# The last norm of a two-layer encoder: tiles read back from DRAM, and a last projection that gives rows

## The chip, the core and the metric

One Trainium2 chip, of which the program uses one core. The metric is the time of one execution in device microseconds. Of the core's engines, TensorE (PE, with its weight loads as PEld) multiplies, VectorE (DVE), ScalarE (ACT) and GpSimd (POOL) work on elements, and SyncE (SP) issues most transfers.

## The reference, cut to what matters

Two groups of sequences, one of 256 and one of 1024 tokens of 1024 features, get 16 learned tokens in front and pass through two layers with shared weights; everything is float32. What matters here is the second half of a layer and the end:

```
h = h + conv_ffn(rmsnorm(h, norm_ffn_g[layer]), w_up[layer], conv_w, conv_b, w_down[layer])
...
def conv_ffn(h, w_up, conv_w, conv_b, w_down):      # D_FF = 2816
    u = dwconv(h @ w_up, conv_w, conv_b, 1)         # width 3, along the tokens
    a, g = u[..., :D_FF], u[..., D_FF:]
    return (gelu(g) * a) @ w_down
...
h = rmsnorm(h, final_norm_g)                        # after the last layer, over the 1024 features
return h[:, N_META:]                                # the 16 learned tokens are dropped
```

## The kernel before

All tokens of both groups lie in one row of 1316 columns, and the residual `h` is kept transposed: features on partitions, in 8 blocks of 128, tokens along the free axis. Its home in DRAM is `hsp` (128 x 8 x 1316). A matmul in float32 is made of three in a rounded format (`mm3`, L237): high times high, high times low, low times high, each operand having been split into a high and a low part.

`ffn` (L301) runs once a layer, and `last` marks the second. It takes the tokens in two halves (`s`), each of two quarters, `ca` and `cb`, of 328 or 330 columns (`QO`, L59). The up projection of a block of two 128-wide strips and two quarters is done with seven products in place of eight (`pair`, L430; 12 matmuls a product, L456); POOL and ACT prepare the sums of weights and split them (`part`, `supply`, L331 to L367), eight products ahead. `inputs` (L373) prepares the token side for a whole half, in tiles of the pool `xs` (seven buffers). In a half, the first two pairs run interleaved (L568 to L577); `take` (L539) fetches the two quarters' residual tiles `hs` there. Then come ten turns, f0 = 2 to 20 (L579): a pair of the first kind (`hold`), `down` for the two strips before in both quarters, the load of the next two `w_down` units (`down_units`, L510), and a pair of the second kind (`gate`), which makes the activations `xa`.

`down` (L519) takes slices of `w_down` as the stationary operand and activations as the moving one: for each of the 8 feature blocks six matmuls of 328 or 330 columns into one of the PSUM banks a, b, c, d (two buffers each, taken in turn), and VectorE adds the result to `hs` (L526). After the turns, one `down` for each quarter is still due (`end`, L562). In the first layer `give` (L544) then stores `hs` to `hsp` from ACT's queue; in the second it does nothing. The first layer's second half also fetches its first half back (`again`, L548), for the next norm.

The final norm is done by jobs (`final`, L620) of up to 128 tokens, three a quarter: 8 transposes from `hs` into two banks (L632), two squares with sums on ACT (L635), the sum and the inverse root on DVE and POOL (L636, `rstd` L193), two scalings on DVE (L640) and a store from SP (L642). The scaled rows go into `hs` itself, over columns that were just transposed; a job of fewer than 128 tokens uses the columns of the job before (`home`, L1652 to L1653). The four quarters' jobs run at four places: quarter 0 between blocks of the first half's last `down` (L604), quarter 1 among the interleaved pairs of the second half (L567, L573), quarter 2 between blocks of the very last `down` (L610), quarter 3 after it (L611).

The order on TensorE is the program's (L1710 opens a manual schedule for it); the other engines' and SP's orders come from the scheduler's own timing of the program, which may put an instruction ahead of others that are written earlier.

Of the kernel before, what the change touches and what calls it, by code (L numbers as in the profile page):

```python
# [91 lines left out]
class Trunk:  # L92
# [208 lines left out]
    def ffn(self, l, p_norm, hn, h1, right):  # L301
# [242 lines left out]
        def give(c):  # L544
            if not last:
                self.store(self.hsp[:, :, QO[c][0]:QO[c][0] + QO[c][1]], hs[c][:, :, :QO[c][1]], True)
# [16 lines left out]
        for s in range(2):  # L563
# [3 lines left out]
            jobs = iter(self.final(fg, hs, (1,), "cd") if s and last else ())  # L567
            for i in range(7):  # L568
                for j, product, follow in pairs:
                    step(product, j, i)  # L570
                    follow(i)
                if i < 3:
                    next(jobs, lambda: None)()  # L573
                if i == 1:
                    take(ca)
                if i == (3 if s else 1):
                    take(cb)  # L577
            down_units(0)
            for f0 in range(2, NF, 2):  # L579
# [7 lines left out]
                elif s and not last and f0 in (6, 10):  # L587
                    behind = {2: [call(hfactors, f0 // 4 - 1)], 5: [call(hspread, f0 // 4 - 1)]}
                run_pair(ja, s, X, hold, behind)
# [7 lines left out]
            if not s:  # L597
# [6 lines left out]
                down(end, cb, {m: [f] for m, f in zip((1, 4, 7), self.final(fg, hs, (0,), "ab"))} if last else {})  # L604
                give(cb)
        left.close()
        if last:
            down(end, ca)
            fg = self.final_weights(self.wsp, "wlo")
            down(end, cb, {m: [f] for m, f in zip((1, 4, 7), self.final(fg, hs, (2,), "ab"))})  # L610
            for f in self.final(fg, hs, (3,), "ab"):  # L611
                f()
            return
# [1006 lines left out]
    def final(self, fg, hs, quarters, banks):  # L1620


        nc, v = self.nc, self.nc.vector

        def job(c, x, home, out, t, n):
            y = hs[c][:n, :, home:home + 128]
            ss = self.nrm.tile([128, 4], F32, tag="ss", name="ss", bufs=2)
            halves = []
            for g in range(2):
                ps = self.bank(banks, (128, 4, 128))  # L1630
                for k in range(4):
                    nc.tensor.transpose(ps[:n, k, :], hs[c][:, 4 * g + k, x:x + n], self.ident)
                halves.append(ps[:n])
            for g in range(2):
                nc.scalar.activation(out=y[:, 4 * g:4 * g + 4], in_=halves[g], func=AF.Square, accum_out=ss[:n, g:g + 1])
            v.tensor_tensor(out=ss[:n, 2:3], in0=ss[:n, 0:1], in1=ss[:n, 1:2], op=ALU.add)
            self.rstd(ss[:n, 3:4], ss[:n, 2:3])
            for g in range(2):
                q = slice(4 * g, 4 * g + 4)
                v.scalar_tensor_tensor(out=y[:, q], in0=halves[g], scalar=ss[:n, 3:4],  # L1640
                                       in1=fg[:n].rearrange("p (k x) -> p k x", x=128)[:, q], op0=ALU.mult, op1=ALU.mult)
            self.dma(out[0, t:t + n, :].rearrange("t (k x) -> t k x", x=128), y)

        jobs = []
        for c in quarters:
            c0, n = QO[c]
            home = None
            for col, out, count in ((COLA + NM, self.o["out_0"], TA - NM), (COLB + NM, self.o["out_1"], TB - NM)):
                a, b = max(col, c0), min(col + count, c0 + n)
                for x in range(a, b, 128):  # L1650
                    m = min(128, b - x)
                    if home is None or m == 128:  # L1652
                        home = x - c0  # L1653
                    jobs.append(lambda c=c, x=x - c0, home=home, out=out, t=x - col, m=m: job(c, x, home, out, t, m))
        return jobs
# [89 lines left out]
```

## Time and profile before

| | us |
|---|---|
| median of 3 executions | 3126.32 (3125.46 to 3127.15) |
| the profiled execution | 3126.3 |
| its span, first to last instruction | 3124.2 |
| TensorE busy in the span | 2830.4 (91%) |
| VectorE, ScalarE, GpSimd busy | 2031.4, 1505.7, 1704.5 |
| mean granted TensorE clock | 0.955 |

The rows that follow the change come from several views of this one execution. In a timeline a row is one instruction or several alike in sequence: start, length, engine, line of the kernel, operation, tile written and tiles read, shape; behind it, in brackets, how long the engine stood idle before it and what ended that. A matmul's length includes its drain, which the next one overlaps, so that the price of one in a stream is the distance between two starts. In the table of stretches, the columns are the length, then for each engine the busy time and the number of instructions, the granted clock as a share of the full one, the DMA engines' busy share and the GB/s.

### The profile page before, as it was taken

The numbers are of one execution on the slowest core, as the hardware profiler recorded it, in microseconds if no ns is written. First come the engines' busy times: TensorE is split into PE (matmuls) and PEld (weight loads), VectorE is DVE, ScalarE is ACT, GpSimd is POOL, SyncE is SP. The second block draws the span as 40 slices with busy tenths as digits, with TensorE's granted clock in tenths as the row PEclk, the third lists the DMA queues.
The fourth block names the chain that finished last, engine by engine and source line by source line (L and its number), as shares of the span: only waits on it lengthen the run. The fifth ranks groups of instructions, "written<-read, shape, count | busy, mean of one in ns | idle before, by whom it ended". The sixth has DMA issues, their size and how long they took to land. (4 is left out here: it accounts for less than half of the span.)

```text
span 3124.2 us, 48747 instructions
## 1 busy us (share of the span) xinstructions
PE 2830.4 (91%) x17937; PEld 2712.1 (87%) x17937; DVE 2031.4 (65%) x4210; ACT 1505.7 (48%) x2909; POOL 1704.5 (55%) x1438
## 2 busy tenths in 40 slices
PE   6999757879999989999989998897999996999995
PEld 5988536879999989999978887787999996999995
DVE  8998793256666686666664777757655566666663
ACT  5445782244444454444444666634444444444442
POOL 1000100068888877788714333327888884788871
PEclk9999877989999999999999999998999998999997
DMA  5332543242222252222247667664222223222211
GB/s 146 85 87 57 129 124 116 76 134 75 81 82 82 82 180 84 68 77 80 75 129 168 142 145 158 158 186 156 80 77 79 80 85 107 85 82 82 82 55 49
DMA packets 407693, 320.22 MB, mean 102 GB/s; under 512 B 39262, under 2 KB 384270, under 8 KB 407454
## 3 DMA queue, kind: packets, MB, share of 16 engines
q1 hardware_dynamic: 357502, 260.01, 29.0%
q0 software_dynamic: 35520, 32.89, 5.3%
q10 hardware_dynamic: 14432, 24.20, 2.2%
q8 instruction: 142, 2.33, 0.3%
q14 instruction: 97, 0.79, 0.1%
HBM read 257.82 MB, written 57.11 MB: 101 GB/s over the span
## 5 line engine op out<-in xcount | busy, mean ns | idle before, releaser
L516 POOL TENSOR_TENSOR dl<-rawd,dh 128x1024 fp32r<-128x1024 f32 x88 | 213.3, 2424 | 311.5 <-ACT dh L515 311.4
L248 PE MATMUL ps_a<-hh,whi 128*128 128x438 f32 (+5 forms) x848 | 295.2, 348 | 43.7 <-ACT hh L1160 27.1
L515 ACT CAST dh<-rawd 128x1024 fp32r<-128x1024 f32 x88 | 92.3, 1048 | 436.4 <-PE ps_d L249 421.2
L249 PE MATMUL ps_a<-hl,whi 128*128 128x438 f32 (+5 forms) x848 | 290.2, 342 | 3.0 <-DVE hl L1504 2.3
L253 PE MATMUL ps_a<-hh,wlo 128*128 128x438 f32 (+5 forms) x848 | 288.7, 341 | 0.0
L338 POOL TENSOR_TENSOR s<-raw 128x512 f32<-128x512 f32 x184 | 257.6, 1402 | 29.9 <-PE ps_d L253 25.4
L365 POOL TENSOR_TENSOR wlo<-s,wlo 128x512 fp32r<-128x512 f32 x176 | 235.7, 1340 | 16.5 <-ACT wlo L364 15.1
L365 POOL TENSOR_TENSOR whi<-s,whi 128x512 fp32r<-128x512 f32 x176 | 235.2, 1346 | 3.8 <-ACT whi L364 3.8
L364 ACT CAST wlo<-s 128x512 fp32r<-128x512 f32 x176 | 108.9, 620 | 229.5 <-PE ps_a L456 97.0
L248 PEld LDWEIGHTS ps_a<-hh,whi 128*128 128x128 f32 x848 | 165.1, 195 | 55.4 <-ACT hh L1160 27.8
L365 POOL TENSOR_TENSOR whi<-raw,whi 128x512 fp32r<-128x512 f32 x132 | 176.2, 1336 | 65.3 <-ACT whi L364 65.2
L456 PE MATMUL ps_c<-x,wlo 128*128 128x330 f32 (+1 forms) x1152 | 195.3, 319 | 11.1 <-DVE hs L1640 7.5
L456 PE MATMUL ps_a<-x,whi 128*128 128x330 f32 (+1 forms) x1104 | 187.6, 319 | 11.7 <-DVE x L1513 4.5
L456 PE MATMUL ps_d<-x,whi 128*128 128x330 f32 (+1 forms) x1104 | 188.1, 319 | 6.8 <-DVE x L1513 3.0
L456 PEld LDWEIGHTS ps_c<-x,wlo 128*128 128x128 f32 x1152 | 181.7, 193 | 11.9 <-issue 7.7
L456 PE MATMUL ps_d<-x,wlo 128*128 128x330 f32 (+1 forms) x1008 | 171.7, 320 | 15.9 <-ACT wlo L364 6.7
L456 PEld LDWEIGHTS ps_a<-x,whi 128*128 128x128 f32 x1104 | 174.5, 192 | 13.0 <-DVE x L1513 5.0
L456 PEld LDWEIGHTS ps_d<-x,whi 128*128 128x128 f32 x1104 | 174.5, 192 | 8.7 <-DVE x L1513 3.6
L456 PEld LDWEIGHTS ps_d<-x,wlo 128*128 128x128 f32 x1008 | 159.6, 193 | 18.3 <-ACT wlo L364 7.3
L456 PE MATMUL ps_a<-x,wlo 128*128 128x330 f32 (+1 forms) x1008 | 169.2, 317 | 5.0 <-DVE hs L1640 4.2
L365 POOL TENSOR_TENSOR wlo<-raw,wlo 128x512 fp32r<-128x512 f32 x132 | 171.6, 1312 | 1.4 <-ACT wlo L364 1.3
L249 PEld LDWEIGHTS ps_a<-hl,whi 128*128 128x128 f32 x848 | 164.7, 194 | 8.7 <-DVE hl L1504 2.6
(498 smaller groups left out, 8769.0 us busy)
## 6 DMA issues: line engine op xcount, KB each, us to landing
raw<-in_w_up SPq DMA_DIRECT2D x176, 512.0 KB
rawd<-in_w_down SPq DMA_DIRECT2D x88, 512.0 KB
qs<-st SPq DMA_DIRECT2D x48, 219.0 KB
q<-qs POOLq DMA_DIRECT2D x80, 128.0 KB, 3.8
raw<-in_w_out_ab SPq DMA_DIRECT2D x16, 512.0 KB
raw<-in_w_o SPq DMA_DIRECT2D x16, 512.0 KB
hs<-hsp SPq DMA_DIRECT2D x6, 1312.0 KB
raw<-in_w_in_ab SPq DMA_DIRECT2D x12, 512.0 KB
```

Of the source, the lines that this page charges most:

```text
L248: yield nc.tensor.matmul(ps, ah, bh, start=(j == 0), stop=False)
L249: yield nc.tensor.matmul(ps, ah, bl, start=False, stop=False)
L253: yield nc.tensor.matmul(ps, al, bh, start=False, stop=(j == n - 1))
L338: nc.gpsimd.tensor_tensor(out=out, in0=a, in1=b, op=op)
L364: nc.scalar.copy(w[:, 0], src)
L365: nc.gpsimd.tensor_tensor(out=w[:, 1], in0=src, in1=w[:, 0].bitcast(F32), op=ALU.subtract)
L456: nc.tensor.matmul(ps[b], w[:, e, k * 128:(k + 1) * 128], x[:, f, k, :n], start=(opens and k == 0 and y == 0), stop=(k == 3 and y == 2), s ...
L515: nc.scalar.copy(hi, raw)
L516: nc.gpsimd.tensor_tensor(out=lo, in0=raw, in1=hi.bitcast(F32), op=ALU.subtract)
```

## The change

- `give` stores in the second layer too, so that after the first half quarters 0 and 1 go to `hsp`, as in the first layer. No norm job runs in the last `down` of the first half or among the interleaved pairs.
- In the second half six jobs, for the tiles of quarters 0 and 1, run one a turn in turns f0 = 4 to 14, after the last product of the first pair. A job fetches its tile from `hsp` into a part of a free `xs` tile, transposes it into banks a and b, and finishes as before (`finish`); its scaled rows go into another part of the same tile.
- The last `down` is not called in the second half. In its place, for each tile of up to 128 tokens of quarters 2 and 3, and for each half of the features, the activations are the stationary operand and a `w_down` unit is the moving one, 512 columns at a time, so that rows of tokens come out; four products of `hs` with the identity add the residual into the same bank. Then `finish` works from the banks, with its result in a tile of its own in `wsp` (four buffers).
- `final_norm_g` is loaded once.

```diff
--- before.py
+++ after.py
@@ -542,8 +542,7 @@
             self.dma(hs[c][:, :, :QO[c][1]], self.hsp[:, :, QO[c][0]:QO[c][0] + QO[c][1]])
 
         def give(c):
-            if not last:
-                self.store(self.hsp[:, :, QO[c][0]:QO[c][0] + QO[c][1]], hs[c][:, :, :QO[c][1]], True)
+            self.store(self.hsp[:, :, QO[c][0]:QO[c][0] + QO[c][1]], hs[c][:, :, :QO[c][1]], True)
 
         def again(c):
 
@@ -564,13 +563,12 @@
             j0 = len(up) * s
             ca, cb = 2 * s, 2 * s + 1
             pairs = [(j0, *pair(j0, s, X, hold)), (j0 + 1, *pair(j0 + 1, s, X, gate))]
-            jobs = iter(self.final(fg, hs, (1,), "cd") if s and last else ())
+
+            jobs = iter(self.final(fg, (0, 1), xtile().rearrange("p a k n -> p (a k n)").bitcast(F32)) if s and last else ())
             for i in range(7):
                 for j, product, follow in pairs:
                     step(product, j, i)
                     follow(i)
-                if i < 3:
-                    next(jobs, lambda: None)()
                 if i == 1:
                     take(ca)
                 if i == (3 if s else 1):
@@ -586,6 +584,8 @@
                     again(f0 // 4 - 1)
                 elif s and not last and f0 in (6, 10):
                     behind = {2: [call(hfactors, f0 // 4 - 1)], 5: [call(hspread, f0 // 4 - 1)]}
+                elif s and last and f0 > 2:
+                    behind = {6: [next(jobs, lambda: None)]}
                 run_pair(ja, s, X, hold, behind)
                 down(f0 - 2, ca)
                 down(f0 - 2, cb)
@@ -601,16 +601,23 @@
                 X = inputs(first, ya, yb, 332, tuple(gated))
                 down(end, ca)
                 give(ca)
-                down(end, cb, {m: [f] for m, f in zip((1, 4, 7), self.final(fg, hs, (0,), "ab"))} if last else {})
+                down(end, cb)
                 give(cb)
+        if last:
+            for c in (ca, cb):
+                for x, out, t, n in self.rows(c):
+                    halves = []
+                    for g in range(2):
+                        ps = self.bank("abcd")[:n]
+                        q = slice(512 * g, 512 * g + 512)
+                        self.mm3(ps, [(*(a[:, x:x + n] for a in acts[y, c % 2]), *(u[:, q] for u in units[end + y])) for y in range(2)],
+                                 [(ps[:, 128 * k:128 * k + 128], hs[c][:, 4 * g + k, x:x + n], self.ident) for k in range(4)])
+                        halves.append(ps.rearrange("p (k x) -> p k x", k=4))
+                    y = self.wsp.tile([128, 1024], FR, tag="whi", name="y").bitcast(F32)
+                    self.finish(fg, halves, y[:n].rearrange("p (k x) -> p k x", k=KD), out, t, n)
+            left.close()
+            return
         left.close()
-        if last:
-            down(end, ca)
-            fg = self.final_weights(self.wsp, "wlo")
-            down(end, cb, {m: [f] for m, f in zip((1, 4, 7), self.final(fg, hs, (2,), "ab"))})
-            for f in self.final(fg, hs, (3,), "ab"):
-                f()
-            return
         self.split_tiles(pool(hn, "hn1"))
 
         def apply(c):
@@ -1617,42 +1624,44 @@
         self.dma(fg, self.i["final_norm_g"].rearrange("(o d) -> o d", o=1).to_broadcast([128, D]))
         return fg
 
-    def final(self, fg, hs, quarters, banks):
-
+    def rows(self, c):
+
+        c0, n = QO[c]
+        for col, out, count in ((COLA + NM, self.o["out_0"], TA - NM), (COLB + NM, self.o["out_1"], TB - NM)):
+            a, b = max(col, c0), min(col + count, c0 + n)
+            for x in range(a, b, 128):
+                yield x - c0, out, x - col, min(128, b - x)
+
+    def finish(self, fg, halves, y, out, t, n):
 
         nc, v = self.nc, self.nc.vector
-
-        def job(c, x, home, out, t, n):
-            y = hs[c][:n, :, home:home + 128]
-            ss = self.nrm.tile([128, 4], F32, tag="ss", name="ss", bufs=2)
+        ss = self.nrm.tile([128, 4], F32, tag="ss", name="ss", bufs=2)
+        for g in range(2):
+            nc.scalar.activation(out=y[:, 4 * g:4 * g + 4], in_=halves[g], func=AF.Square, accum_out=ss[:n, g:g + 1])
+        v.tensor_tensor(out=ss[:n, 2:3], in0=ss[:n, 0:1], in1=ss[:n, 1:2], op=ALU.add)
+        self.rstd(ss[:n, 3:4], ss[:n, 2:3])
+        for g in range(2):
+            q = slice(4 * g, 4 * g + 4)
+            v.scalar_tensor_tensor(out=y[:, q], in0=halves[g], scalar=ss[:n, 3:4],
+                                   in1=fg[:n].rearrange("p (k x) -> p k x", x=128)[:, q], op0=ALU.mult, op1=ALU.mult)
+        self.dma(out[0, t:t + n, :].rearrange("t (k x) -> t k x", x=128), y)
+
+    def final(self, fg, quarters, room):
+
+
+        h, y = (room[:, a:a + 1024].rearrange("p (k x) -> p k x", k=KD) for a in (0, 1280))
+
+        def job(c, x, out, t, n):
+            self.dma(h[:, :, :n], self.hsp[:, :, QO[c][0] + x:QO[c][0] + x + n])
             halves = []
             for g in range(2):
-                ps = self.bank(banks, (128, 4, 128))
+                ps = self.bank("ab", (128, 4, 128))
                 for k in range(4):
-                    nc.tensor.transpose(ps[:n, k, :], hs[c][:, 4 * g + k, x:x + n], self.ident)
+                    self.nc.tensor.transpose(ps[:n, k, :], h[:, 4 * g + k, :n], self.ident)
                 halves.append(ps[:n])
...
-        jobs = []
-        for c in quarters:
-            c0, n = QO[c]
-            home = None
-            for col, out, count in ((COLA + NM, self.o["out_0"], TA - NM), (COLB + NM, self.o["out_1"], TB - NM)):
-                a, b = max(col, c0), min(col + count, c0 + n)
-                for x in range(a, b, 128):
-                    m = min(128, b - x)
-                    if home is None or m == 128:
-                        home = x - c0
-                    jobs.append(lambda c=c, x=x - c0, home=home, out=out, t=x - col, m=m: job(c, x, home, out, t, m))
-        return jobs
+            self.finish(fg, halves, y[:n], out, t, n)
+
+        return [lambda c=c, r=r: job(c, *r) for c in quarters for r in self.rows(c)]
 
     def mix(self, es):
 
```

## Rows read from the trace of the kernel before

**Rows 1.** The head of the page: busy time by engine, and TensorE in 40 slices.

```profile
PE 2830.4 (91%) x17937; PEld 2712.1 (87%) x17937; DVE 2031.4 (65%) x4210; ACT 1505.7 (48%) x2909; POOL 1704.5 (55%) x1438
...
PE   6999757879999989999989998897999996999995
```

**Rows 2.** Table of stretches; numbers behind an engine are busy us.

```profile
core 0: us, PE busy (x) PEld busy (x) DVE busy (x) ACT busy (x) POOL busy (x), PEclk, DMA share, GB/s
1109.60:1180.10 70.50, 59.99 (x350) 57.97 (x349) 62.97 (x94) 36.88 (x65) 56.44 (x36) 0.90 0.55 175
2583.10:2678.00 94.90, 68.87 (x398) 65.63 (x397) 65.63 (x112) 42.20 (x81) 51.38 (x43) 0.84 0.35 106
2692.60:2732.60 40.00, 40.00 (x267) 40.00 (x266) 23.95 (x50) 18.60 (x35) 32.49 (x24) 1.00 0.27 80
...
3085.30:3107.10 21.80, 5.75 (x33) 4.76 (x31) 8.10 (x19) 5.04 (x16) 2.20 (x4) 0.66 0.30 87
3107.10:3124.20 17.10, 0.00 (x0) 0.00 (x0) 0.00 (x0) 0.00 (x0) 0.00 (x0) 0.50 0.06 17
```

**Rows 3.** Timeline of TensorE, second layer, where its two halves meet.

```profile
2613.39 1.07 PE L1632 MATMUL ps_b<-ident,hs 128*39 128x128 f32 x4 [4.88 <-DVE hs L526]
...
2626.18 3.69 PE L456 MATMUL ps_a<-x,wlo 128*128 128x332 f32 x12 [4.21 <-DVE hs L1640]
...
2649.97 0.62 PE L456 MATMUL ps_c<-x,wlo 128*128 128x332 f32 x1 [7.46 <-DVE hs L1640]
```

**Rows 4.** Timeline of ScalarE and VectorE near the end.

```profile
3060.24 1.05 ACT L515 CAST dh<-rawd 128x1024 fp32r<-128x1024 f32 x1 [5.25 <-DMA rawd<-in_w_down]
...
3103.29 0.59 ACT L1635 ACTIVATE hs<-ps_a 73x512 f32<-73x512 f32 x1 [6.36 <-DMA out<-hs]
...
3103.87 0.58 ACT L1635 ACTIVATE hs<-ps_b 73x512 f32<-73x512 f32 x1
...
3106.34 0.74 DVE L1640 SCALAR_TENSOR_TENSOR hs<-ps_b,ss,wlo 73x512 f32<-73x512 f32 x1
```

**Rows 5.** Timeline of SP: loads issued, first layer, then second layer.

```profile
1150.47 0.52 SPq L113 DMA_DIRECT2D x<-hsp  x1
...
1166.93 0.52 SPq L113 DMA_DIRECT2D x<-hsp  x1
...
2799.88 1.63 SPq L113 DMA_DIRECT2D raw<-in_w_up  x2
...
3055.68 0.33 SPq L113 DMA_DIRECT2D rawd<-in_w_down  x1
```

**Rows 6.** Timeline of TensorE, first layer, second half's first ordinary pair.

```profile
1168.32 3.69 PE L456 MATMUL ps_a<-x,whi 128*128 128x332 f32 x12 [3.10 <-ACT u L465]
```

**Rows 7.** Timeline of TensorE elsewhere: products by the identity, wide matmuls, transposes.

```profile
553.21 0.78 PE L252 MATMUL ps_a<-ident,xr 128*128 128x128 f32 x6
...
1873.42 0.40 PE L1328 MATMUL ps_d<-th,vv 128*128 128x512 f32 x1
1873.65 0.39 PE L1328 MATMUL ps_d<-tl,vv 128*128 128x512 f32 x1
...
2796.20 2.00 PE L456 MATMUL ps_d<-x,whi 128*128 128x332 f32 x12
...
3077.32 0.60 PE L1632 MATMUL ps_a<-ident,hs 128*128 128x128 f32 x4
3077.76 0.60 PE L1632 MATMUL ps_b<-ident,hs 128*128 128x128 f32 x4
```

**Rows 8.** Timeline of GpSimd in the pair loop.

```profile
2773.30 2.40 POOL L516 TENSOR_TENSOR dl<-rawd,dh 128x1024 fp32r<-128x1024 f32 x1 [7.06 <-ACT dh L515]
```

**Rows 9.** DMA view, GB/s in 40 slices: last store; a 128-row store; a 71-row load.

```profile
GB/s 0 0 0 13 17 14 21 19 23 19 23 21 21 23 21 21 21 23 21 21 23 21 21 21 23 21 21 21 23 21 21 23 21 21 21 23 2 0 0 0
...
GB/s 0 0 0 0 89 253 300 287 280 300 294 280 294 300 280 287 307 273 294 300 280 287 300 280 287 300 287 287 205 62 0 0 0 0 0 0 0 0 0 0
...
GB/s 346 397 329 333 245 184 110 44 54 40 58 22 36 18 22 32 22 32 18 36 18 22 32 22 32 22 32 18 36 18 22 32 22 32 18 36 18 36 18 22
```

More of the change, by code (lines that the diff above doesn't have):

```diff
@@ L1633, in job @@
                 halves.append(ps[:n])
[L1634 to L1641, printed above, removed]
@@ L1642, in job @@
-            self.dma(out[0, t:t + n, :].rearrange("t (k x) -> t k x", x=128), y)
-        jobs = []
-        for c in quarters:
-            c0, n = QO[c]
-            home = None
-            for col, out, count in ((COLA + NM, self.o["out_0"], TA - NM), (COLB + NM, self.o["out_1"], TB - NM)):
-                a, b = max(col, c0), min(col + count, c0 + n)
-                for x in range(a, b, 128):
-                    m = min(128, b - x)
-                    if home is None or m == 128:
-                        home = x - c0
-                    jobs.append(lambda c=c, x=x - c0, home=home, out=out, t=x - col, m=m: job(c, x, home, out, t, m))
```

## The prediction

> **What bounds the kernel now.** I read the head of the page first [rows 1]: TensorE is busy 91% of the span, and the slices show where it is not: slice 34 (2577 to 2655 us) and the last one, both in the second FFN layer. The table of stretches comes next [rows 2]. In one turn of the pair loop (2692.6 to 2732.6) TensorE is busy 40.00 of 40.00 us at full clock, with VectorE, ScalarE and GpSimd at 24, 19 and 32: TensorE sets that stage's pace, so whatever is added to its order there costs its full length unless something hides it, and nothing does.
>
> The two bad slices hold the final norm. The stretch from the last product of the first half to the end of the first ordinary pair of the second half takes 94.9 us in the second layer; the same stretch of code in the first layer, which stores its tiles and has no norm there, takes 70.5. Both hold the same 96 matmuls of `down` and 252 of the pairs; the second layer has 48 transposes more (398 against 350 records). The timeline of TensorE says what is late [rows 3]: transposes wait 4.88 us for an addition into `hs`, and products wait 4.21 and 7.46 us for the scaled tile of a norm job, since a job's squares and scaling stand behind the operand splits on ScalarE and VectorE. The clock granted there is 0.84 against 0.90 [rows 2].
>
> At the end [rows 2] the last `down` ends at about 3085.3; then 21.8 us pass with TensorE busy 5.75, and then 17.1 us with no engine busy at all. Two things fill the 21.8: the jobs run one behind the other, and the third job of each quarter puts its result where the one before put it, so that it waits for that one's store, 6.36 us at the very end [rows 4]. The 17.1 us are the last store.
>
> **The change, part by part.** The profiled execution took 3126.3 us against the median 3126.32, so the sum is made against 3126.3.
>
> *Start of the second half: -26.1.* With `give` storing and the six norm jobs gone, this stretch becomes the first layer's code. Even if it only matches it: -24.4 (94.9 to 70.5). The added stores are in those 70.5 already, on ScalarE's queue as there. The first layer also fetches its first half back and squares it in this very stretch (fetches at 1150.47 and 1166.93, [rows 5]), and one of its holes, 3.10 us before the product at 1168.32, ends on ScalarE's copy of `u` [rows 6], which stood among those squares. The new code has none of them. Without that hole, and the 0.3 us around it, it would be 67.1; I take half: 68.8. Its other holes, for operand splits, stay. Bounds: -20 (no relief, and 4 us lost to the narrower `t` ring of the last layer) to -31.
>
> *The jobs moved into the pair loop: +7.1.* Six jobs, each after the last product of the first pair of turns f0 = 4 to 14, each 8 transposes. Four transposes take 0.44 us (3077.32 to 3077.76, [rows 7]), so 6 x 0.88 = 5.3 us of TensorE in a stage where it has no slack. The rest of a job is taken by slack: two squares on ScalarE (19 of 40 us busy), some 1.8 us on VectorE (24 of 40, [rows 2]) and one short power on GpSimd, which idles 7.06 us once a turn [rows 8]. What could show: the power queues behind GpSimd's splits of weights, and the scaling behind the additions of `down`, which free its banks. A job holds one of the two `a` and one of the two `b` banks for 0.9 us of transposes and, from the first square to the last scaling, 3.8 us (3103.29 to 3107.08, [rows 4]); meanwhile `down` comes back to `a` every 3.6 us (24 matmuls at 40.00 us / 267, [rows 2]) and has the other buffer. I add 0.3 us a job, between 0 and 2.5: +7.1, bounds +5.3 and +20. Each job's 512 KB fetch joins SP's queue. It waits there only for the transposes of the job before, one turn earlier, and the first layer's two fetches, written in the turns f0 = 4 and 8, were issued before the stretch of f0 = 2 had ended (1180.1); I cost it at nothing. Behind it on SP stand the loads of weights; if that cover goes, the second rival below prices it. The dropped reload of `final_norm_g` and the fetches' bytes lie beside a loop in which the DMA engines are 27% busy [rows 2].
>
> *The last projection and its norm: -9.0.* Before: 96 matmuls of 328 or 330 columns and 48 transposes. After: 12 groups (6 row tiles x 2 halves) of 6 matmuls with 512 columns and 4 plain fp32 products of `hs` with the identity. Of two 512-column matmuls the second starts 0.23 us after the first [rows 7]. A plain fp32 product by the identity leaves two records; six of them, some narrower, take 0.78 us with the drain where four transposes take 0.60 [rows 7], so I take the transposes' 0.11 for a record. A group is 6 x 0.233 + 8 x 0.11 = 2.28 us, the twelve 27.3, and with 0.2 us for the last activations TensorE runs from 3067.2 to 3094.7 without a hole: 8 banks, each given back about 8 us after its group begins. TensorE thus gets some 8 us *more* work than before; the gain is in what follows. Only the last tile's chain is left: the second square starts as the matmul drains (3094.9), and from there to the last scaling was 3.2 us (3103.87 to 3107.08 [rows 4]): 3098.1 instead of 3107.1. With six separate `y` tiles in four buffers no job waits for a store.
>
> *The last store: -1.4.* It carries 73 rows. Before, it ran for the whole 17.1 us at about 21 GB/s [rows 9], while a 128-row store moved at about 290. After, its source is contiguous, so it moves 73 pieces of 4096 bytes instead of 584 of 512. The nearest row is the 71-row load in 4096-byte pieces, 18 to 36 GB/s once the other traffic has ended [rows 9], which for 299 KB at an average near 22 is 13.6 us, against 14.5. I take 13.1, bounds 11.7 and 15.2. The Trainium skill ("DMA: Bandwidth & Descriptors", section "Why a DMA increments its semaphore by 16 and not by 1") says a DMA is spread over the largest number up to 16 that divides its slowest dimension, so 73 rows use one engine whatever the pieces are; the trace agrees (21 against 290 GB/s), and by that rule the term stays near zero. If instead the contiguous rows spread like the 128-row store (290 GB/s, 1 us), it would be about -13; that is a rival below.
>
> **Sum:** -26.1 + 7.1 - 9.0 - 1.4 = -29.4; 3126.3 - 29.4 = **3097 us**.
>
> **Rivals.** (1) *The loop pays*: banks and VectorE are short where the job falls, as the pair's own additions crowd there, and each job costs 2.5 us more: 3097 + 13 = 3110. For it: rows 3, where the same job held products up by 4 us; against: those had the operand splits in front, and the loop has none. Chance 0.12.
> (2) *Slower*: the fetch of a job isn't ahead of its turn. Issued in the order written, it stands behind the two weight loads that go out from 2799.88 to 2801.51 [rows 5], where the pair's last product ended at 2798.2 [rows 7], so about 3.4 us late, and a 512 KB load takes 4.6 us to arrive (issue 3055.68 [rows 5], use 3060.24 [rows 4]): TensorE waits 8 us a job, 48 in all, and likely drops its clock: 3097 + 48 = 3145. It decides from 4.9 us a job on (29.4 / 6). Against it: the first layer's early fetches. Chance 0.08.
> (3) *The start of the second half keeps its holes*, because the splits of the operands and not the jobs are late there; only the 48 transposes go, at half clock about 10 us: 3097 + 16 = 3113. Against it: the first layer, with the same splits, needs 70.5. Chance 0.07.
> (4) *The end gains nothing*: the longer products cost what the shorter tail saves: 3097 + 9 = 3106. Chance 0.05.
> (5) *The last store spreads* over many engines: 3097 - 12 = 3085. Chance 0.04.
>
> **How the numbers follow.** The forecast's own cases (3088 to 3105) have 0.64. The range 3088 to 3112 adds (4) and most of (1), and leaves out (2), (3) and (5). All cases but (2) are faster by over 0.2% (6.3 us, about what a measurement of this kernel can tell from no change): 0.88; within it 0.03, a mild form of (2); slower 0.09.
>
> **What would show it.** Right: the stretch at the start of the second half near 69 us, without scaled tiles among what TensorE waits for; turns with a job near 41 us, the others at 40.0; TensorE without a hole from the last pair to its last matmul, about 27.5 us; about 3.2 us of squares and scaling, then a store of 13 to 15 us as the only thing left. Wrong: transposes that wait for the fetched tile, or a turn with a job of 43 us and more.

## The result, and the profile after

The changed kernel took 3091.72 us (median of 4 runs, 3088.84 to 3096.3) against 3125.89 of the kernel before (4 runs): a ratio of 0.9892, 95% interval 0.9875 to 0.9909, 34 us faster. The prediction said 3097 and a range of 3088 to 3112. The profiled execution took 3088.84 us, with a span of 3086.3.

The head of the page, where the two bad slices of [rows 1] are to be looked for:

```profile
PE 2827.2 (92%) x17961; PEld 2707.1 (88%) x17961; DVE 2029.6 (66%) x4194; ACT 1504.3 (49%) x2909; POOL 1713.2 (56%) x1438
...
PE   6999756879999989999989999887999998999997
```

TensorE has about as much to do as before (2827 us against 2830), so the gain is not work that went away. Slice 34 is at 8 instead of 6, and the last slice at 7 instead of 5.

The table of stretches of the kernel after, in the order: the halves' meeting in the first layer, the same in the second; a loop turn with a job, the turn of the fourth job, a turn without one; the last projection up to its last matmul; the last store. It answers to [rows 2].

```profile
1108.80:1179.30 70.50, 59.98 (x350) 57.97 (x349) 62.95 (x94) 36.86 (x65) 56.44 (x36) 0.90 0.55 175
2579.80:2645.00 65.20, 57.66 (x350) 56.13 (x349) 57.46 (x87) 33.66 (x56) 53.45 (x34) 0.92 0.51 156
2659.67:2700.54 40.87, 40.87 (x275) 40.86 (x274) 25.91 (x54) 20.06 (x39) 33.01 (x25) 1.00 0.36 104
2782.26:2825.19 42.93, 41.32 (x274) 40.82 (x273) 28.42 (x54) 19.61 (x39) 32.99 (x25) 1.00 0.35 99
2906.90:2946.90 40.00, 40.00 (x266) 40.00 (x265) 24.01 (x50) 18.99 (x35) 32.49 (x24) 1.00 0.27 80
3040.50:3067.90 27.40, 27.36 (x170) 22.84 (x168) 12.69 (x30) 10.10 (x28) 2.74 (x5) 1.00 0.18 69
...
3071.80:3086.30 14.50, 0.00 (x0) 0.00 (x0) 0.00 (x0) 0.00 (x0) 0.00 (x0) 0.50 0.06 21
```

From the starts of the last products on either side, the start of the second half went from 94.94 us to 65.29 (-29.65), the rest of the loop from 389.15 to 395.44 (+6.29), and the time from the last pair's last product to the end of the program from 57.17 to 45.93 (-11.24). Together -34.6, where the medians lie 34.2 apart. The second layer now needs 5.3 us less than the first for the same 350 records (65.20 against 70.50 in the table).

At the start of the second half the timeline of TensorE has three waits of over 1 us left, all for the operands' splits; none ends on a scaled tile of a norm job, as two of [rows 3] did:

```profile
2605.52 2.22 PE L456 MATMUL ps_b<-x,whi 128*128 128x332 f32 x11 [1.92 <-DVE x L1520]
2615.99 0.42 PE L456 MATMUL ps_d<-x,whi 128*128 128x332 f32 x1 [1.56 <-ACT x L1519]
2619.45 3.41 PE L456 MATMUL ps_d<-x,whi 128*128 128x332 f32 x11 [3.04 <-DVE x L1520]
```

In the loop the timeline of SP shows the jobs' fetches. The one at 2767.91 is for the tile that TensorE transposes at 2807.90, 40 us later, and the next follows those transposes at once, so that a tile is always fetched a turn ahead:

```profile
2767.91 0.53 SPq L113 DMA_DIRECT2D x<-hsp  x1
...
2808.97 0.53 SPq L113 DMA_DIRECT2D x<-hsp  x1
```

```profile
2807.90 0.60 PE L1660 MATMUL ps_a<-ident,x 128*128 128x128 f32 x4
2808.34 0.60 PE L1660 MATMUL ps_b<-ident,x 128*128 128x128 f32 x4
```

At the end the last square begins as the last matmul drains, the last scaling ends at 3071.56 (3070.82 + 0.74), 3.2 us later, as in [rows 4], and then one store of 73 rows is left. First the timelines of ScalarE and VectorE, then the DMA view of that store (GB/s in 40 slices from 3071 us), which answers to [rows 9]:

```profile
3068.35 0.59 ACT L1640 ACTIVATE y<-ps_d 73x512 f32<-73x512 f32 x1 [1.44 <-PE ps_d L253]
```

```profile
3069.07 0.15 DVE L1641 TENSOR_TENSOR ss<-ss 73x1 f32<-73x1 f32 x1 [1.98 <-ACT y L1640]
...
3070.82 0.74 DVE L1645 SCALAR_TENSOR_TENSOR y<-ps_d,ss,fg 73x512 f32<-73x512 f32 x1
```

```profile
GB/s 0 0 0 21 11 11 21 21 0 21 21 11 32 11 32 21 32 21 32 21 21 32 21 32 21 32 21 32 21 32 21 32 21 21 32 21 21 0 0 0
DMA packets 74, 0.30 MB, mean 20 GB/s; under 512 B 1, under 2 KB 1, under 8 KB 74
```

The 73 pieces still go one behind the other, over 34 slices of 0.38 us, 13.0 us in all.

A warning on small differences: from the last product of the first layer to the first of the second nothing differs between the kernels of this study, and yet that stretch took from 546.8 to 552.4 us in their profiled executions. Parts are therefore compared by their own stretches below; of two medians, differences under some 5 us say little.

### The profile page after: what moved, and what is told of

Its sections match the earlier page's. It is cut to its first block, busy times and chain, and to the rows that moved or that the text cites. A ratio compares the mean times of both kernels' runs of the same rounds, so it can differ in the third digit from the quotient of the medians.

```text
span 3086.3 us, 48784 instructions
## 1 busy us (share of the span) xinstructions
PE 2827.2 (92%) x17961; PEld 2707.1 (88%) x17961; DVE 2029.6 (66%) x4194; ACT 1504.3 (49%) x2909; POOL 1713.2 (56%) x1438
## 4 chain that ended last, share of the span: by engine, by line
PE 69%; DVE 14%; DMA 6%; ACT 4%; POOL 3%; issue 3%; SPq 1%; DVEq 0%; ACTq 0%; POOLq 0%
PE ps_d L456 9%; PE ps_c L456 9%; PE ps_a L456 9%; PE ps_b L456 5%; PE ps_a L248 4%; PE ps_a L253 4%; PE ps_a L249 4%; PE ps_c L248 2%; PE ps_c L253 2%; PE ps_c L249 2%; PE ps_d L248 2%; PE ps_d L253 2%; PE ps_d L249 2%; PE ps_b L248 2%; PE ps_b L253 2%
## 5 line engine op out<-in xcount | busy, mean ns | idle before, releaser
L253 PEld LDWEIGHTS ps_a<-hh,wlo 128*128 128x128 f32 x848 | 163.6, 193 | 5.7 <-issue 2.2
```

The lines of the kernel that those rows point to most:

```text
L253: yield nc.tensor.matmul(ps, al, bh, start=False, stop=(j == n - 1))
```

## The experiments

### The two parts alone

Start and loop of the changed kernel with the old end:

```diff
-        if last:
-            for c in (ca, cb):
-                ...
+        if last:
+            down(end, ca)
+            down(end, cb, {m: [f] for m, f in zip((1, 4, 7), self.final_old(fg, hs, (2,), "ab"))})
+            for f in self.final_old(fg, hs, (3,), "ab"):
+                f()
```

> Changed kernel with the end of the kernel before: `down` of both last quarters with the weights standing, the six transposing jobs, results laid into `hs`. Theory (the three parts are separate and add up): first stretch of the second half 65.3 us as in the changed kernel, loop 395.4, end 57.2 as before; 3126 - 29.7 + 6.3 = 3102 us. Rival (the start gains only together with the new end, because the free room or the schedule differs): the stretch stays above 75 us and the time above 3110.

Measured: 3102.39 us (ratio to before 0.9918, 0.9905 to 0.9932). The table of stretches, start of the second half, then the last projection up to the last scaling, then the last store:

```profile
2584.60:2649.70 65.10, 56.09 (x351) 54.16 (x350) 57.39 (x88) 33.37 (x56) 53.34 (x34) 0.95 0.51 156
3044.80:3084.90 40.10, 23.00 (x147) 21.21 (x145) 21.09 (x50) 10.23 (x30) 3.30 (x6) 0.79 0.20 60
3084.90:3101.60 16.70, 0.00 (x0) 0.00 (x0) 0.01 (x1) 0.00 (x0) 0.00 (x0) 0.50 0.06 18
```

And the new end alone, on the kernel before:

```diff
+        if last:
+            for c in (ca, cb):
+                ...
+            left.close()
+            return
         left.close()
-        if last:
-            down(end, ca)
-            ...
```

> Kernel before with the new end alone: jobs of the first two quarters stay where they were, the last projection has the weights as the moving operand. Theory: stretch 94.9 us and loop 389.2 as before, from the last pair's last product to the program's end 45.9 instead of 57.2; 3126 - 11 = 3115 us. Rival: the end gains nothing by itself (longer products against a shorter tail), 3124 or more.

Measured: 3114.05 us (0.9956, 0.9943 to 0.9968). The same three stretches:

```profile
2582.60:2676.60 94.00, 67.80 (x398) 64.50 (x398) 65.75 (x113) 42.09 (x81) 51.27 (x43) 0.84 0.36 107
3065.30:3096.50 31.20, 27.87 (x171) 22.99 (x169) 14.51 (x34) 10.78 (x30) 3.29 (x6) 1.00 0.20 77
3096.50:3111.30 14.80, 0.00 (x0) 0.00 (x0) 0.00 (x0) 0.00 (x0) 0.00 (x0) 0.53 0.06 20
```

What follows: the parts don't lean on each other. The start is 65 us with either end and 94 without its change; the end is 40.1 + 16.7 with the old code and 31.2 + 14.8 with the new. By the medians the two alone give 25.3 and 13.7 us against the kernel before as measured beside them (3127.73), 39 together against 34 for the whole change, a difference of the size that the warning names. Note in the second column how TensorE's work in the end *rose*, from 23.0 to 27.9 us, while the stretch shrank by 9.

### What pays at the end: the swapped operands, or tiles of their own?

The new end does two things: rows come out of the matmul, and each result has a tile of its own. This kernel does the second alone; it is the first experiment's kernel with one line changed:

```diff
-            y = hs[c][:n, :, home:home + 128]
+            y = self.wsp.tile([128, 1024], FR, tag="whi", name="y").bitcast(F32)[:n].rearrange("p (k x) -> p k x", k=KD)
```

> Changed kernel with the old end (weights standing, 48 transposes), but each job writes its result into a tile of its own instead of into `hs`. Theory A (the two waits of 7.56 and 6.36 us for stores out of `hs` are the whole gain of the end, and the swapped operands cost TensorE more than they give): the last scaling comes about 29 us after the last pair's last product instead of 31.2, the time is 1 to 3 us below the changed kernel, about 3090. Theory B (the swap brings the gain, since rows come out without transposes): the end is 5 us longer or more, 3097 and above.

Measured: 3090.51 us (0.9882, 0.9868 to 0.9895), level with the changed kernel. Last projection up to the last scaling, and last store:

```profile
3041.90:3071.90 30.00, 22.36 (x147) 20.50 (x145) 20.98 (x50) 10.23 (x30) 3.30 (x6) 0.90 0.21 81
3071.90:3086.70 14.80, 0.00 (x0) 0.00 (x0) 0.00 (x0) 0.00 (x0) 0.00 (x0) 0.50 0.06 20
```

The single line is worth 10.1 of the 40.1 us, and it shortens the store as well (16.7 to 14.8), whose source is contiguous with a tile of its own. Theory A holds: the swap of operands, the larger part of the new code, brings nothing here that the separate tiles don't, and with it the last scaling comes 1.2 us later (31.15 us after the last product against 29.98).

### The last store

```diff
-        self.dma(out[0, t:t + n, :].rearrange("t (k x) -> t k x", x=128), y)
+        for a, b in ((0, n // 16 * 16), (n // 16 * 16, n)):
+            if a < b:
+                self.dma(out[0, t + a:t + b, :].rearrange("t (k x) -> t k x", x=128), y[a:b])
```

> Changed kernel, each store of 72 or 73 rows cut in two, of 64 rows and of 8 or 9. Theory (a store of 73 rows goes through one engine because no number from 2 to 16 divides 73, as the Trainium skill has it in "DMA: Bandwidth & Descriptors", and its 73 pieces of 4096 bytes run one behind the other at 0.155 us): the 64 rows spread over 16 engines and the 9 over nine, the last store ends some 2.5 us after its issue instead of 13.5; 11 us less, 3081 us. Rival (the pieces are slow because of where they go, or both parts end on one engine): no change, 3092.

Measured: 3080.80 us (0.9854, 0.9839 to 0.9869), 11 us below the changed kernel. The DMA view from 3072.2 us to the end (4.2 us, so a slice is 0.1 us), and the stretch:

```profile
DMA  0000000000995995993795161000000000000000
GB/s 0 0 0 0 0 0 0 0 0 0 234 312 117 273 234 117 234 273 78 156 351 156 39 235 39 0 0 0 0 0 0 0 0 0 0 0 0 0 0 0
```

```profile
3072.20:3076.40 4.20, 0.00 (x0) 0.00 (x0) 0.00 (x0) 0.00 (x0) 0.00 (x0) 0.50 0.32 71
```

The same bytes move in some 1.6 us (16 slices) at around 200 GB/s, where the one store of 73 rows needed 13.0 us. The rule of the Trainium skill that the prediction used ("DMA: Bandwidth & Descriptors", section "Why a DMA increments its semaphore by 16 and not by 1") is borne out from both sides: 73 rows, a count that no number from 2 to 16 divides, went through one engine although they were contiguous, and the cut into 64 and 9 rows spread.

### Why the start is shorter than the first layer's

```diff
         def again(c):
 
             hs[c] = fetch(QO[c])
-            square(c)
+            square(c, after=gated[0])
...
-                nc.scalar.activation(out=sq, in_=h(c, k), func=AF.Square)
+                x = nc.scalar.activation(out=sq, in_=h(c, k), func=AF.Square); after and self.order(x.ins, after)
```

> Changed kernel; in the first layer the squares of the first half are ordered behind the turn's last copy into `xa`, so that none stands among the work of the second half's first two pairs. The order on TensorE is the same. Theory (the squares held up ScalarE's copy of `u` and made the first layer's stretch longer than the second layer's is now): the first layer's stretch falls from 70.5 us to between 65.3 (the second layer's) and 67.1 (without the one hole of 3.10), the squares find room later; 3 to 5 us less, 3087 to 3089. Rival (the hole has another cause, such as the additions into `hs`): the stretch stays at 69 us or more, the time within 1.5 us of the changed kernel.

Measured: 3083.43 us (0.9861, 0.9844 to 0.9879); the first layer's stretch is 65.06 us. The timeline of TensorE at the place of [rows 6], first of the changed kernel, then with the squares late:

```profile
1167.54 3.69 PE L456 MATMUL ps_a<-x,whi 128*128 128x332 f32 x12 [3.11 <-ACT u L465]
1171.03 3.06 PE L456 MATMUL ps_c<-x,wlo 128*128 128x332 f32 x12
```

```profile
1167.26 2.08 PE L456 MATMUL ps_a<-x,whi 128*128 128x332 f32 x12 [0.33 <-ACT u L465]
1169.17 1.97 PE L456 MATMUL ps_c<-x,wlo 128*128 128x332 f32 x12
```

And the table of stretches of the changed kernel over that hole and what follows (the number behind POOL's is the granted clock):

```profile
1164.46:1167.54 3.08, 0.00 (x1) 0.01 (x1) 3.08 (x6) 2.30 (x5) 3.08 (x3) 0.84 0.30 84
1167.54:1171.30 3.76, 3.76 (x13) 3.76 (x14) 3.76 (x8) 1.02 (x3) 3.76 (x4) 0.50 1.01 340
```

The squares were the whole difference, and the hole cost more than its length: 2.8 us of waiting (3.11 - 0.33), and then two groups of 12 products at a granted clock of 0.50, which is 1.2 GHz, 1.6 and 1.1 us slower (3.69 and 3.06 against 2.08 and 1.97). That is 5.5, and the stretch lost 5.4. The squares found room in the loop, whose length changed by -0.7 us; that is a balance, for by the starts of the first products two of its turns became 1.4 us longer and one 4.0 shorter, and no run separates those. Stretch and loop make 6.1 us; the medians differ by 8.3, more than the 3 to 5 expected, and what lies between is within the spread told of above.

### What stood in the way at the start of the kernel before

```diff
                 halves.append(ps[:n])
+            if c < 2:
+                return
             for g in range(2):
```

> Kernel before; of the jobs of the first two quarters only the transposes are left (their squares, sums, powers, scalings and stores are left out, so those rows are not written). Theory (what made the start of the second half long was the jobs' squares and scalings ahead of the operands' splits on ScalarE and VectorE): the stretch falls from 94.9 us to 65.3 and the 48 transposes, 5.3 us at full clock and some 10 at half: 71 to 76; 3126 - 21 = 3105 us. Rival (the transposes themselves do it, since they wait for the additions into `hs` in TensorE's order and break its run): the stretch stays above 85 us, 3116 or more.

Measured: 3100.18 us (0.9919, 0.9905 to 0.9933). The stretch, by its last products 67.21 us:

```profile
2581.50:2648.70 67.20, 62.25 (x398) 60.18 (x398) 55.26 (x89) 31.98 (x53) 47.42 (x32) 0.95 0.34 104
```

All 398 records are there, and the stretch is only 1.9 us longer than without the transposes: they fall where TensorE waits anyway. So 27.7 of the 29.65 us went with what the jobs do behind their transposes (squares, sums, powers, scalings and stores) and with the banks that they hold until it is done. The third rival falls, and the expectation of 71 to 76 was too cautious in the same direction.

The run takes all of that away at once and doesn't tell which part weighed most. On the two waits of [rows 3] that end on a scaled tile, the timelines of ScalarE and VectorE of the kernel before say more:

```profile
2623.03 0.59 ACT L1635 ACTIVATE hs<-ps_a 39x512 f32<-39x512 f32 x1 [4.64 <-DMA out<-hs]
...
2644.31 0.59 ACT L1635 ACTIVATE hs<-ps_c 72x512 f32<-72x512 f32 x1 [1.15 <-DMA out<-hs]
```

```profile
2649.07 0.75 DVE L1640 SCALAR_TENSOR_TENSOR hs<-ps_c,ss,fg 72x512 f32<-72x512 f32 x1 [2.79 <-POOL ss L197]
```

Both belong to the third job of a quarter, of 39 and 72 rows, and the product, which reads no scaled tile, waits for the bank that this job's scaling reads. The job's squares had to wait until the store of the job before had left `hs`, and in the second case VectorE then waited for the power, which stood behind sums and splits of weights on GpSimd. So the wait for stores, which the prediction saw at the end alone, was here too. Whether a tile of its own for each job, with the jobs left where they were, would have given back a part of the 27.7 us, no run tried.

### What a job costs in the loop

```diff
-            jobs = iter(self.final(fg, (0, 1), ...) if s and last else ())
+            jobs = iter(())
```

> Changed kernel without the six jobs in the pair loop (the rows of the first two quarters are not normalized and not written); the tiles are still stored to DRAM. Theory (a job costs its eight transposes, 0.86 us, and nothing else): all turns 40.0 us, the loop 5.2 us shorter, 3086.5 us; 2 us less again if the one turn of 42.93 us was a job's too. Rival 1 of the prediction (a job also takes banks and VectorE from the pair): 10 us less or more. The start of the second half stays at 65.3 us, whether or not a job's room is taken from the operands' tiles.

Measured: 3084.04 us (0.9866, 0.9851 to 0.9881); the loop 388.34 us instead of 395.44. The jobs cost 7.1 us: 6 x 0.86 for their transposes (40.87 against 40.00 a turn), and 2 us in the fourth job's turn alone. The start stayed at 65.03.

### The fetch without its turn of lead

```diff
-            self.dma(h[:, :, :n], self.hsp[:, :, QO[c][0] + x:QO[c][0] + x + n])
+            self.order(self.nc.scalar.dma_start(out=h[:, :, :n], in_=self.hsp[:, :, QO[c][0] + x:QO[c][0] + x + n]).ins, self.conv)
```

(`self.conv` names the last activation of `convolve`.)

> Changed kernel with the fetch of each loop job issued on ScalarE's queue behind the last activation of the pair before it, instead of a turn ahead on SP's. The order on TensorE is the same. Theory (the fetch is hidden only because it goes out a turn ahead; the prediction's rival 2 priced it otherwise at 8 us a job): TensorE's transposes wait for the tile about 5 to 8 us a job, 30 to 48 us more, 3122 to 3140 us. Rival (DRAM to the tile is short enough, or the waits are taken back in the same turn by work that is ahead): less than 2 us a job, 3104 or less.

Measured: 3134.04 us, *slower* than the kernel before (1.0021, 1.0011 to 1.0031). The loop took 434.66 us, 39.2 more than in the changed kernel, 6.5 a job. From the groups of the line of the transposes, what ended TensorE's idle time before them, and from its timeline one of them:

```profile
  DMA x<-hsp: 28.8, 6
```

```profile
2745.96 1.09 PE L1660 MATMUL ps_a<-ident,x 128*128 128x128 f32 x4 [5.68 <-DMA x<-hsp]
```

4.8 us a job are the wait itself; four transposes then take 1.09 us instead of 0.60, and the loop's granted clock is 0.96 instead of 1.00. This is the second rival's mechanism with its sign: one DMA's place on a queue decides whether the whole change is a gain.

### The fourth job's turn

That turn took 42.6 to 43.5 us in each of the five profiled executions that had the jobs' fetches ahead and their sum on VectorE. The timelines of VectorE and GpSimd of the changed kernel show what was late:

```profile
2810.29 3.62 DVE L1641 TENSOR_TENSOR ss<-ss 128x1 f32<-128x1 f32 x1
2813.95 0.15 DVE L196 TENSOR_SCALAR ss<-ss 128x1 f32<-128x1 f32 x1
```

```profile
2810.08 1.33 POOL L338 TENSOR_TENSOR s<-raw,s 128x512 f32<-128x512 f32 x1
2811.33 1.33 POOL L338 TENSOR_TENSOR s<-raw 128x512 f32<-128x512 f32 x1
2812.58 1.32 POOL L365 TENSOR_TENSOR whi<-raw,whi 128x512 fp32r<-128x512 f32 x1
2814.18 0.55 POOL L197 TENSOR_TENSOR ss<-ss,mhalf 128x1 f32<-128x1 f32 x1 [0.28 <-DVE ss L196]
```

An addition of one column, 0.15 us at the end of the program (3069.07 above), lasts until 2813.91, and GpSimd's chain of back-to-back instructions ends at 2813.90, where its next one, the power, needs this very sum. In the other five turns with a job the same addition was held up too, but only to the end of the one GpSimd instruction that was running (0.67 to 0.68 us). The same timelines in the first of these turns, where the last row of VectorE is one with an operand in PSUM:

```profile
2687.50 0.68 DVE L1641 TENSOR_TENSOR ss<-ss 128x1 f32<-128x1 f32 x1
...
2688.29 0.55 DVE L427 SCALAR_TENSOR_TENSOR a<-ps_d,cw,a 128x330 f32<-128x330 f32 x1
```

```profile
2686.88 1.29 POOL L338 TENSOR_TENSOR s<-raw,s 128x512 f32<-128x512 f32 x1
2688.13 1.30 POOL L338 TENSOR_TENSOR s<-raw 128x512 f32<-128x512 f32 x1
```

There the addition ended at 2688.18, as one GpSimd instruction gave way to the next, with no gap between them. Why the fourth was let in only at the third such place is not known. So the sum went to ScalarE:

```diff
-        v.tensor_tensor(out=ss[:n, 2:3], in0=ss[:n, 0:1], in1=ss[:n, 1:2], op=ALU.add)
+        nc.scalar.activation(out=ss[:n, 2:3], in_=ss[:n, 0:1], func=AF.Identity, scale=1.0, bias=ss[:n, 1:2])
```

> Changed kernel; the one-column sum of a job's two halves is made by ScalarE (an activation with the other half as its bias) instead of by VectorE, whose instruction reads two operands from SBUF. Theory (in the fourth loop job that addition, 0.16 us elsewhere, lasted 3.5 to 3.6 us in every run with jobs, until GpSimd had its first gap, so VectorE's two-operand read was kept out by GpSimd's reads, as the Trainium skill has it in "SBUF — State Buffer", "Who interferes with whom"): no such row is left, the fourth job's turn falls from 42.6 to 42.9 us to 40.9 like the others, the loop is 2 us shorter, some 3090 us. Rival (the instruction was late for another reason, or the next one on VectorE takes the delay over): the fourth turn stays at 42.5 or more.

Measured: 3091.02 us (0.9889, 0.9874 to 0.9904). The fourth job's turn:

```profile
2783.40:2824.30 40.90, 40.90 (x275) 40.88 (x274) 25.35 (x53) 19.89 (x39) 33.02 (x25) 1.00 0.36 104
```

The turn is like the others, and the loop 2.2 us shorter (393.27). The whole time does not show it: 2 us is below what the medians tell apart.

### All together, and the old end once more

The changed kernel with the three edits above:

```diff
+            square(c, after=gated[0])
...
+        nc.scalar.activation(out=ss[:n, 2:3], in_=ss[:n, 0:1], func=AF.Identity, scale=1.0, bias=ss[:n, 1:2])
...
+        for a, b in ((0, n // 16 * 16), (n // 16 * 16, n)):
```

> Changed kernel with the stores cut in two (e4), the first layer's squares late (e5) and the sum on ScalarE (e9). If the three are separate: 3091.7 - 11 - 6 - 2 = 3073 us. If they share something (the first layer's stretch or the last store hides part of another): above 3077.

Measured: 3073.77 us (0.9835, 0.9820 to 0.9851), as the sum of the parts had it: 65.04 us for the first layer's stretch, 65.14 for the second's, 393.32 for the loop, 35.53 for the end. It beats both kernels.

Since the swap of operands brought nothing, its undoing was tried on top, with the scalings ordered so that no job waits out the power of its own sum:

```diff
-            for c in (ca, cb):
-                ...
+            down(end, ca)
+            down(end, cb, {m: [lambda r=r: tail(ca, *r)] for m, r in zip((1, 4, 7), self.rows(ca))})
...
+                ps = self.bank("abcd", (128, 4, 128))
...
+                later and self.order(x.ins, self.mean)
```

> The kernel of e10 with the old end (weights standing, 48 transposes, results in tiles of their own, eight banks), and each scaling of the last quarter ordered behind the next job's mean. Theory (the swap of operands is not what pays; TensorE does less without it, and what held the old end up besides its stores was VectorE waiting out each job's power by itself, 2.42 us a job): the last scaling ends 27 us after the last pair's last product instead of 31.2, 4 us below e10, 3069 us. Rival (the swap is as good or better once the stores are out of the way): 3072 or more.

Measured: 3073.55 us (0.9834, 0.9816 to 0.9853): not the 4 us. The last scaling ended 30.4 us after the last product, not 27. The timeline of ScalarE has the reason:

```profile
3058.02 0.60 ACT L1646 ACTIVATE y<-ps_a 128x512 f32<-128x512 f32 x1 [1.58 <-DVE ss L196]
...
3061.30 0.59 ACT L1646 ACTIVATE y<-ps_c 73x512 f32<-73x512 f32 x1 [1.69 <-DVE y L1652]
```

The squares of the last two jobs wait for the column of sums of two jobs before, of which there are two.

```diff
-        ss = self.nrm.tile([128, 4], F32, tag="ss", name="ss", bufs=2)
+        ss = self.nrm.tile([128, 4], F32, tag="ss", name="ss", bufs=4)
```

> The kernel of e11 with four buffers instead of two for a job's column of sums (`ss`). Theory (in e11 the swap's undoing failed to pay only because the last squares waited on ScalarE, twice 1.6 us, for VectorE to be done with the column of two jobs before): both waits go, the last scaling ends 27 us after the last pair's last product instead of 30.4, 3 us below e11 in the same stretch; the time about 3070 us. Rival (another wait takes their place, a bank or a tile for the result): the stretch stays within 1 us of e11's.

Measured: 3072.31 us (0.9825, 0.9807 to 0.9842). Both waits are gone, and the stretch from the last product to the last scaling is 27.9 us, 2.5 below the kernel before it and 3.4 below the one with the swap (31.28):

```profile
3038.40:3066.30 27.90, 20.57 (x146) 19.77 (x144) 19.94 (x44) 11.32 (x36) 3.28 (x6) 0.94 0.21 75
2946.40:2986.60 40.20, 40.20 (x266) 40.20 (x265) 24.02 (x50) 18.92 (x34) 32.48 (x25) 1.00 0.26 79
```

The mechanism is right, but the medians of these last three kernels differ by 1.5 us with intervals that overlap, so which is fastest stays open. In this profiled execution every turn without a job took 40.20 us instead of 40.00 (second line) at the same clock, and so did undisturbed turns of the first layer's second half, where no job runs at all; the cause isn't known.

## Why the prediction was right, and where its terms were off

- **What bounds the kernel** held: TensorE sets the loop's pace (the eight transposes of a job cost their full length, 0.86 us against the 0.88 of the sum), and waits set the two bad slices.
- **Start of the second half, -26.1; measured -29.65.** The direction and the basis (the first layer's same code) were right. The step that was off is "Without that hole, and the 0.3 us around it, it would be 67.1; I take half: 68.8". The squares were the cause of that hole, wholly and not half, and the hole's price was 5.4 us rather than 3.4, because the products behind it ran at half the clock. The stretch came out at 65.3; with the squares late the first layer comes out at 65.1. The reason that the prediction gave for the waits of [rows 3], squares and scaling behind the operand splits, was incomplete: both waits for scaled tiles shown there hold a wait of the third job for a store out of `hs` (4.64 and 1.15 us), and the longer one 2.79 us for a power on GpSimd as well.
- **Jobs in the loop, +7.1; measured +6.3.** The transposes, 5.3 in the sum, came out at 5.2. The allowance of 0.3 us a job did not come as banks or additions running short: five jobs cost nothing beside their transposes, and the fourth 2 us, for a reason that the prediction did not have. Without jobs the loop is 0.8 us below that of the kernel before, which makes up the difference. The fetches' cost of nothing was right. The fourth turn all but met the sign set for being wrong, a turn of 43 us and more (42.93 here, 43.5 with the store cut in two); it came without the 2.5 us in every job that the first rival spoke of.
- **Last projection and norm, -9.0; measured -8.9** (40.03 to 31.15 us from the last product to the end of the last scaling). TensorE ran 27.4 us without a hole of note, and the chain behind it took 3.2. But the sentence "TensorE thus gets some 8 us more work than before; the gain is in what follows" was only half an answer: TensorE's busy time rose by 4.9 us, what follows was shortened by the separate tiles, and the additional work bought nothing. That the term was met to 0.1 us is therefore no proof of the swap.
- **Last store, -1.4; measured -2.4** (17.14 us from the last scaling to the end, then 14.78). One engine, as said, and its 73 pieces took 13.0 us against the 13.1 taken. The other us lies around the packets, and no run tells where from.
- **Sum, -29.4; measured -34.6** by the stretches; of the 5.2 between them the start has 3.5, the last store 1.0 and the loop 0.8. Before the changed code the profiled execution was 3.3 us ahead of the one before (2582.96 to 2579.69 at the end of the first half), which is the spread told of above and no part of the change. The three terms that were off all erred to the cautious side, so nothing cancelled, and the time came out 5 us below the forecast.
- **The rivals.** The first (2.5 us a job) fell: five of six turns paid the transposes alone. The second was the right danger: with the lead of the fetch taken away (here by issuing it late on ScalarE's queue, not behind loads on SP's), the measured 39.2 us of loop and a kernel slower than before stand beside its 48. The third fell with the transposes left in place, 67.2 us. The fourth fell, the end gave 11.2. The fifth fell for the change as it is, and a store cut in two shows the 11 us that it spoke of.

## What to carry to other kernels

Look at what a stretch's *other* engines hold in front of the bounding engine's operands: here 27.7 of 29.7 us went with short side jobs, their work among the operands' splits and the banks that they held, and in a stage where those engines have slack they cost the bounding engine's own 0.86 us each and 2 us in one turn, as long as their loads go out a turn ahead. When a rewrite changes two things at once, try the smaller alone: one line that gave each result a tile of its own did all that the rewritten projection did. Price a hole before TensorE with the clock of what follows it, and look at the number of rows of the last store before anything else in a tail.

## What the runs showed of the hardware

- A one-column addition on VectorE with both operands in SBUF lasted 0.15 us at the end of the program, with GpSimd idle, and 0.67 to 0.68 us in five turns of the loop, each time to the end of the GpSimd instruction that was running. In the fourth job's turn it lasted 3.62 us, from 2810.29 to 2813.91, and outlasted the GpSimd instruction that was running and two more that began after it. VectorE's instructions with an operand in PSUM took their usual time beside GpSimd (0.55 us at 2688.29). The Trainium skill ("SBUF — State Buffer", section "Who interferes with whom") says that a VectorE instruction with two SBUF inputs contends with a GpSimd instruction that reads SBUF; the trace agrees, and adds that the wait can go on over several of them. With the sum on ScalarE there was no such row. What it is that the two engines share was not measured separately.
- A hole of 3.1 us before TensorE was followed by 24 products at a granted clock of 0.50, which cost 2.7 us more; without the hole they ran at full speed.
- 73 pieces of 4096 bytes in one store moved in 13.0 us, with a DMA share of 0.06, which is one engine of 16; 64 and 9 rows in two stores took about 1.6 us together, as seen in the DMA view.
